# Element-wise work of a transformer kernel moved from GpSimd to the vector engine

## The chip, the cores and the metric

The kernel runs as one launch on one core of a Trainium2 chip. The core's engines work side by side, each through its own instruction queue: TensorE (PE) multiplies matrices, VectorE (DVE), ScalarE (ACT) and GpSimd (POOL) do element-wise work, and SyncE (SP) issues the weight transfers. The metric is the time of one execution in microseconds; several executions are told by their median, lowest and highest.

## The reference

Everything is float32, for 256 positions of width 1024. A first block has two layers `x + W_out(y)`, in which `y` joins four gated mixers (a 31-wide convolution, a 3-wide one, windowed attention, neighbourhood attention with a relative bias). A second block has two layers of feed-forward, mixing, feed-forward; its mixing joins a forgetting attention, a dilated attention and a gated recurrence (HGRN2). Cut to what the change touches:

```python
def rmsnorm(x, g):                       # before every stage
    y = x32 * lax.rsqrt(jnp.mean(x32 * x32, axis=-1, keepdims=True) + EPS)
y_b = short_gated_conv(b_b, b_c, b_x, conv_b_w) * jax.nn.silu(b_z)      # gate, one of four
scores = jnp.where(col_ok[:, None, :], scores + bias[None], NEG_INF)    # neighbourhood attention
out = jnp.concatenate([x1 * cos - x2 * sin, x2 * cos + x1 * sin, rest]) # rotary
def step(S, inp):                        # the recurrence, chunk by chunk
    q, k, v, lf = inp
    b = jnp.cumsum(lf, axis=2)
    D = jnp.exp(jnp.where(causal, b[:, :, :, None, :] - b[:, :, None, :, :], NEG_BIG))
    A = jnp.einsum('bhtse,bhse->bhts', q[:, :, :, None, :] * D, k)
    intra = jnp.einsum('bhts,bhsv->bhtv', A, v)
```

## The kernel before

Activations lie in SBUF with features on the 128 partitions and the 256 positions along the free axis; a width of 1024 is 8 slices of 128x256. Weights stream from HBM in pieces of up to 1 MB (`ws`) through SyncE's queue into three tiles `st`. To keep float32 accuracy on fp32r matmuls, each weight piece and each activation is split in a high and a low part, and every product is the sum of three matmuls (`hi` with `hi`, `hi` with `lo`, `lo` with `hi`). `hi` is an ACT copy of `st`. `lo` is either one DVE subtraction (`lo<-st,hi`, by `tt`), or ACT writes the negative of `hi` into `lo` and a DMA issued on POOL's queue (L592) adds `st` to it.

The stages follow each other: mixing of the first block (0 to 157 us and 157 to 298), then for each layer of the second block a feed-forward, a mixing and a feed-forward (298, 484, 640 and 826, 1010, 1166 to the end). A mixing is an input projection, element-wise work on its results, and an output projection.

**What sets the order.** The program is written as generators, each yielding operations (`Op`) and waits; a list scheduler (`Scheduler.step`) repeatedly takes the operation with the smallest estimated start, less a priority, by a table of costs of its own, and emits it. So each engine's instructions stand in one fixed order, and an engine waits at the instruction that is next. `V`, `A`, `G` put an operation on DVE, ACT, POOL; `tt`, `ts`, `stt` are DVE operations; `VG` allows DVE or POOL and leaves the choice to that estimate. Helpers emit everything, so that ACT's work is at L472, DVE's and POOL's at L495, the softmax's custom DVE operations at L526.

**What the change touches.**
- `prep`: the sum of squares for the next norm. Each of 8 slices is squared (`sq`, by ACT; on POOL before the first stage) and added to `sqa` (L805, `G`).
- `rope`: rotary, a product with `sinp` and an addition (`VG`).
- `biases` in the first block's mixing: the bias table `nb` is loaded, scaled by 8 (DVE), and a column mask is added (POOL), 4 times per layer.
- `z`: the gate's product `y` (`VG` where its coefficient is 1).
- `hf`: two subtractions of the forget gate (`VG`).
- `recurrence` and `level`: eight levels per layer. For each, ACT takes `e = exp(sp)` (tile `lev`, 128x1024), one of three buffers. Behind it two DVE additions update `sp` for the next level in place (`sp<-sp`, 128x512 each). Beside them `level` multiplies `lev` by `kq` (the product `lev<-lev,kq`, 128x1024, `VG`), PE forms small blocks from it (L546, for the last two levels L535), and DVE copies these into `at` under a mask (L1490, COPY_PREDICATED), ACT for the last levels. All eight done, PE forms the outputs from `at` and `hv`.

Round the recurrence stand, on the same engines, the forgetting attention (softmax tiles `pt`, with `fb`), the rotary (`u`, `ak`, `aq`), the dilated attention (its `pt` from `cst`), and the weights' splits.

Of the kernel before, what the change touches and what calls it, by code (L numbers as in the profile page):

```python
# [14 lines left out]
ALU = mybir.AluOpType  # L15
PSUM = bass.MemoryType.PSUM

P = 128
T = 256
# [380 lines left out]
class Builder:  # L400
# [380 lines left out]
    def prep(self, st, fo):  # L781

        yield self.xin[fo]
        xs = self.x[:, fo]
        g = st["g"][:, fo:fo + 1]
        if st["act"]:
            hi, lo, _ = st["pair"]
            yield self.A(hi[:, fo], xs, AF.Copy, scale=g)
            yield self.stt(lo[:, fo], xs, g, hi[:, fo].bitcast(F32), ALU.mult, ALU.subtract)
        st["ready"][fo].done = True  # L790
        if fo:
            yield st["summed"][fo - 1]
        for i, sc in enumerate(st["sq_scale"]):
            sq = yield (("sqa",) if fo == 0 else ("sq",))
            if st["first"]:
                yield self.G("tensor_tensor", sq, xs, xs, op=ALU.mult)
            else:
                yield self.A(sq, xs, AF.Square, scale=1.0 if sc is None else sc[:, fo:fo + 1])
            if fo == 0:
                st["acc"][i] = sq  # L800
            elif fo == KT - 1:
                st["last"][i] = sq
            else:
                a = st["acc"][i]
                yield self.G("tensor_tensor", a, a, sq, op=ALU.add)  # L805
                self.s.put("sq", sq)
        st["summed"][fo].done = True

# [219 lines left out]
    def rope(self, bank, ps, nf, cos, sin, o, tags):  # L1028


        s = self.s
        a, b = yield tags
        av, bv = a[:, :nf], b[:, :nf]
        for i in range(4):
            j = i ^ 1
            yield self.A(bv[32 * i:32 * i + 32], ps[32 * j:32 * j + 32], AF.Copy)
        yield self.tt(av, ps, cos[:, None, :].to_broadcast([P, nf, T]), ALU.mult)
        s.put("acc", bank)
        yield self.VG("tensor_tensor", bv, bv, sin[:, None, :].to_broadcast([P, nf, T]), op=ALU.mult)
        yield self.VG("tensor_tensor", o, av, bv, op=ALU.add)  # L1040
        s.put(tags[0], a)
        s.put(tags[1], b)


    def mix_a(self, l, st, nxt):
        nc, tc, s = self.nc, self.tc, self.s
        done = Event()
        with tc.tile_pool(name="mixa", bufs=1, reuse_waits="tile") as mp:
# [16 lines left out]
            def biases():  # L1065
                yield self.have_ct
                for b in range(2):
                    for h in range(4):
                        src = bass.AP(tensor=self.rpb.tensor,
                                      offset=self.rpb.offset + (l * 4 + h) * 465 + (5 - b) * 31 + 15 - 63,  # L1070
                                      ap=[[1, 64], [31, 6], [1, 64]])
                        yield self.DMA(nb[b * 64:b * 64 + 64, h], src, 98304)
                nb3 = nb.rearrange("p h u c -> p (h u) c")
                for h in range(4):
                    n1 = nb[:, h]
                    yield self.ts(n1, n1, 8.0, None, ALU.mult)
                    yield self.G("tensor_tensor", n1, n1, self.c["nacol"][:, None, :].to_broadcast([P, 6, 64]), op=ALU.add)
                E["bias"].done = True

            def small():  # L1080
# [144 lines left out]
            def z(o, ev, coef, k0, rev=False):  # L1225
                def f_(bank, ps):
                    th, gz = yield ("th", "gz")
                    yield self.A(th, ps, AF.Tanh, scale=0.5)
                    yield self.stt(gz, th, 1.0, ps, ALU.add, ALU.mult)
                    s.put("acc", bank)  # L1230
                    s.put("th", th)
                    yield E[ev]
                    y = yield ("y",)
                    for f in range(2):
                        a, b, c = y[:, f], o[:, f], gz[:, f]
                        if rev:
                            r = lambda q: q.rearrange("p (r c) -> p r c", c=64)
                            a, b, c = r(a), r(b)[:, :, ::-1], r(c)
                        if coef != 1.0:
                            yield self.stt(a, b, coef, c, ALU.mult, ALU.mult)  # L1240
                        else:
                            yield self.VG("tensor_tensor", a, b, c, op=ALU.mult)
                    s.put("gz", gz)
                    yield from emit(k0, y)
                    s.put("y", y)
                return f_
# [124 lines left out]
    def mix_b(self, l, st, nxt):  # L1371
        nc, tc, s = self.nc, self.tc, self.s
        done = Event()
        with tc.tile_pool(name="mixb", bufs=1, reuse_waits="tile") as mp:
# [42 lines left out]
            def hf(c):  # L1417
                def f_(bank, ps):
                    yield self.bconsts
                    h0 = 4 * l + 2 * c  # L1420
                    e, a = yield from log1p_exp(ps, 2, self.nlncol[:, h0:h0 + 2])
                    u, t1 = yield ("u", "u")
                    yield self.stt(u, ps, 0.0, a[:, 0], ALU.max, ALU.add)
                    yield self.stt(t1, ps, 0.0, a[:, 0], ALU.min, ALU.subtract)
                    for j in range(2):
                        h = 2 * c + j
                        yield self.A(kq[:, 0, h * T:h * T + T], u[:, j], AF.Exp, scale=-1.0,
                                     bias=self.l1mcol[:, h0 + j:h0 + j + 1])
                    for j in range(2):
                        yield self.ts(u[:, j], ps[:, j], self.lncol[:, h0 + j:h0 + j + 1], 0.0, ALU.subtract, ALU.min)  # L1430
                    s.put("acc", bank)
                    yield self.VG("tensor_tensor", u, u, a[:, 1], op=ALU.subtract)
                    s.put("lev", e)
                    yield self.VG("tensor_tensor", sp_[:, 1, c * 512:c * 512 + 512].rearrange("p (a b) -> p a b", a=2),
                                  t1, u, op=ALU.subtract)
                    s.put("u", u)
                    s.put("u", t1)
                    E[f"hf{c}"].done = True
                return f_
# [14 lines left out]
            def mixed(tl, m):  # L1454

                return bass.AP(tensor=tl.tensor, offset=tl.offset,
                               ap=[list(tl.ap[0]), [2 * m, D // (2 * m)], [D + m, 2], [1, m]])
# [22 lines left out]
            def level(lev, e):  # L1480
                m = 1 << lev
                ev = e.rearrange("p (b two m) -> p b two m", two=2, m=m)
                yield self.VG("tensor_tensor", ev, ev, mixed(kq, m), op=ALU.mult)
                bank = yield ("sm",)
                if m < 64:
                    for t in range(2):
                        yield blocks(bank, t, e, e)
                    yield box["lev"][lev]
                    mk = self.msk[:, lev * 64:lev * 64 + 64][:, None, :].to_broadcast([P, 8, 64])
                    yield Op([("V", .602, lambda: self.nc.vector.copy_predicated(atc, mk, b8(bank)))],  # L1490
                             [extent(atc)], [extent(bank), extent(self.msk)])
                    if m == 32:
                        for b in range(2):
                            bs = slice(64 * b, 64 * b + 64)
                            yield self.A(at[bs, 0:2, :, bs], atc[bs].rearrange("p (t h) j -> p t h j", t=2), AF.Copy)
                elif m == 64:
                    for h in range(4):
                        yield self.MMs([(b8(bank)[64 * t:64 * t + 64, h], e[:, h * T + t * P:h * T + t * P + 64],
                                         e[:, h * T + t * P + 64:h * T + t * P + P], True, True) for t in range(2)])
                    yield box["lev"][lev]  # L1500
                    for t in range(2):
                        yield self.A(at[:64, t, :, 64:], b8(bank)[64 * t:64 * t + 64, :4], AF.Copy)
                else:
                    pa = bank.rearrange("p (h t) -> p h t", h=4)
                    for h in range(4):
                        yield self.MM(pa[:, h], e[:, h * T:h * T + P], e[:, h * T + P:h * T + T])
                    yield box["lev"][lev]
                    yield self.A(at[:, 2], pa, AF.Copy)
                s.put("sm", bank)
                s.put("lev", e)  # L1510
                box["lev"][lev + 1].done = True
# [386 lines left out]
```

## Time and profile before

| | |
|---|---|
| median of 3 executions | 1361.81 us (1359.84 to 1370.74) |
| profiled execution | 1359.77 us, of which the span 1358.0 us |
| PE busy | 1277.9 us, 94% of the span |
| DVE busy | 865.0 us, 64%, 1481 instructions |
| ACT busy | 921.3 us, 68%, 1420 instructions |
| POOL busy | 320.1 us, 24%, 318 instructions |

The span runs from the first to the last instruction. The profile gives, for every instruction, start, duration, and what ended the idle time of its engine before it. A share of busy time is a mean over stages with different limits, so the stages have to be looked at one by one. A duration holds also time in which an instruction had started and could not go on, so that one operation of one shape can show very different durations.

### The profile page before, as it was taken

The numbers are of one execution on the slowest core, as the hardware profiler recorded it, in microseconds if no ns is written. First come the engines' busy times: TensorE is split into PE (matmuls) and PEld (weight loads), VectorE is DVE, ScalarE is ACT, GpSimd is POOL, SyncE is SP. The second block draws the span as 40 slices with busy tenths as digits, with TensorE's granted clock in tenths as the row PEclk, the third lists the DMA queues.
The fourth block names the chain that finished last, engine by engine and source line by source line (L and its number), as shares of the span: only waits on it lengthen the run. The fifth ranks groups of instructions, "written<-read, shape, count | busy, mean of one in ns | idle before, by whom it ended". The sixth has DMA issues, their size and how long they took to land.

```text
span 1358.0 us, 21863 instructions
## 1 busy us (share of the span) xinstructions
PE 1277.9 (94%) x8530; PEld 1144.4 (84%) x8530; DVE 865.0 (64%) x1481; ACT 921.3 (68%) x1420; POOL 320.1 (24%) x318
## 2 busy tenths in 40 slices
PE   6899988999999999789999999999999888999997
PEld 5888887888888898678888888888899776888886
DVE  6586658569966556856666556666555785666632
ACT  5487748777686578587666656666559767766652
POOL 4222312242121112512222112222121340322211
PEclk9899998999999999899999999999999899999998
DMA  8887988798777779255877777777778645877771
GB/s 262 229 234 203 231 237 232 204 241 271 224 235 240 236 219 256 82 171 156 263 233 234 228 230 228 225 240 237 239 232 230 180 104 161 236 243 242 236 226 53
DMA packets 59783, 294.09 MB, mean 217 GB/s; under 512 B 12448, under 2 KB 14240, under 8 KB 34208
## 3 DMA queue, kind: packets, MB, share of 16 engines
q1 hardware_dynamic: 39232, 219.01, 45.3%
q0 software_dynamic: 20448, 73.69, 28.5%
q8 instruction: 67, 1.10, 0.3%
q14 instruction: 36, 0.29, 0.1%
HBM read 217.94 MB, written 1.05 MB: 161 GB/s over the span
## 4 chain that ended last, share of the span: by engine, by line
PE 70%; ACT 10%; DVE 7%; DMA 7%; issue 3%; POOL 2%; SPq 0%; POOLq 0%; DVEq 0%; ACTq 0%
PE bank L576 34%; PE bank L577 19%; PE bank L579 4%; DMA lo<-st 3%; DVE sp L495 3%; ACT hi L472 3%; DMA st<-ws 3%; PE bank L563 2%; PE bank L565 2%; PE bank L564 2%; ACT lev L472 2%; PE bank L535 2%; ACT lo L472 1%; PE bank L546 1%; ACT pt L472 1%
## 5 line engine op out<-in xcount | busy, mean ns | idle before, releaser
L576 PE MATMUL bank<-act,hi 128*128 128x512 f32 x1456 | 520.0, 395 | 2.3 <-DVE act L495 2.3
L472 ACT ACTIVATE hi<-st 128x1024 fp32r<-128x1024 f32 (+3 forms) x416 | 428.6, 1036 | 80.6 <-DMA st<-ws 39.2
L577 PE MATMUL bank<-act,lo 128*128 128x256 f32 x1664 | 433.4, 281 | 0.6 <-ACT act L472 0.6
L495 DVE TENSOR_TENSOR lo<-st,hi 128x1024 fp32r<-128x1024 f32 (+1 forms) x274 | 338.0, 1237 | 133.5 <-ACT hi L472 130.1
L577 PEld LDWEIGHTS bank<-act,lo 128*128 128x128 f32 x1664 | 312.8, 188 | 18.6 <-ACT act L472 0.9
L576 PEld LDWEIGHTS bank<-act,hi 128*128 128x128 f32 x1456 | 273.6, 188 | 57.8 <-DVE act L495 3.8
L592 POOL DMA_DIRECT2D lo<-st x142 | 123.9, 873 | 652.2 <-ACT lo L472 524.1
L576 PE MATMUL bank<-ha,hi 128*128 128x512 f32 x672 | 236.7, 394 | 0.0
L565 PE MATMUL bank<-act,lo 128*128 128x256 f32 x720 | 208.9, 290 | 24.9 <-DMA lo<-st 24.9
L563 PE MATMUL bank<-act,hi 128*128 128x256 f32 x720 | 214.1, 297 | 0.0
L564 PE MATMUL bank<-act,hi 128*128 128x256 f32 x720 | 207.7, 288 | 0.0
L577 PE MATMUL bank<-ha,lo 128*128 128x256 f32 x704 | 192.7, 281 | 0.0
L565 PEld LDWEIGHTS bank<-act,lo 128*128 128x128 f32 x720 | 141.7, 197 | 26.1 <-DMA lo<-st 26.1
L472 ACT ACTIVATE lo<-hi 128x1024 fp32r<-128x1024 f32 (+1 forms) x142 | 149.3, 1052 | 3.8
L576 PEld LDWEIGHTS bank<-ha,hi 128*128 128x128 f32 x672 | 126.2, 188 | 27.0
L563 PEld LDWEIGHTS bank<-act,hi 128*128 128x128 f32 x720 | 142.1, 197 | 5.9 <-issue 5.0
L564 PEld LDWEIGHTS bank<-act,hi 128*128 128x128 f32 x720 | 141.4, 196 | 0.1
L577 PEld LDWEIGHTS bank<-ha,lo 128*128 128x128 f32 x704 | 132.4, 188 | 2.7
L495 POOL TENSOR_TENSOR fs<-fs,rbc 128x512 f32<-128x512 f32 x44 | 64.0, 1456 | 179.4 <-ACT fs L472 179.4
L495 DVE SCALAR_TENSOR_TENSOR x<-bank,x 128x256 f32<-128x256 f32 x128 | 53.6, 422 | 58.6 <-PE bank L579 56.7
L495 DVE TENSOR_TENSOR fh<-bank,fh 128x256 f32<-128x256 f32 x88 | 37.1, 423 | 76.6 <-ACT fh L472 76.6
L579 PE MATMUL bank<-act,hi 128*128 128x512 f32 x208 | 82.2, 395 | 0.1
(216 smaller groups left out, 1543.8 us busy)
## 6 DMA issues: line engine op xcount, KB each, us to landing
st<-ws SPq DMA_DIRECT2D x197, 1024.0 KB, 5.0
lo<-st POOLq DMA_DIRECT2D x136, 512.0 KB, 5.7
st<-ws SPq DMA_DIRECT2D x2, 1040.0 KB, 7.1
st<-ws SPq DMA_DIRECT2D x4, 512.0 KB, 7.4
st<-ws SPq DMA_DIRECT2D x8, 192.0 KB, 5.3
nb<-rpb SPq DMA_DIRECT2D x16, 96.0 KB, 7.5
st<-ws SPq DMA_DIRECT2D x2, 768.0 KB, 6.5
lo<-st POOLq DMA_DIRECT2D x2, 520.0 KB, 6.7
```

The costliest lines, as they stand in the source:

```text
L472: return Op([("A", dur, lambda: self.nc.scalar.activation(out, in_, func, **kw))], outs, ins, ACT_SETS.get(func))
L495: return (eng, dur, lambda: fn(out, *ins, **kw)), [extent(a) for a in aps]
L535: return Op([("P", dur, lambda: self.nc.tensor.matmul(out, lhsT, rhs, start=start, stop=stop))], [extent(out)], [extent(lhsT), extent(rhs)])
L546: mm(o, l, r, start=st, stop=sp)
L563: mm(out, ah, bh, start=first, stop=False)
L564: mm(out, ah, bl, start=False, stop=False)
L565: mm(out, al, bh, start=False, stop=last)
L576: mm(out, wh, x, start=first, stop=False)
L577: mm(out[:, 0], wl, x[:, 0], start=False, stop=False)
L579: mm(out, wh, x, start=False, stop=True)
L592: return Op([("G", ADD_ISSUE, lambda: self.nc.gpsimd.dma_start(out, src, accum_op=ALU.add))], [extent(out)], [extent(src), extent(out)], l ...
```

## The change

Five places name DVE where GpSimd or the scheduler's choice stood, and the table's two operations become one (`stt`: times 8, plus mask).

```diff
--- before.py
+++ after.py
@@ -802,7 +802,7 @@
                 st["last"][i] = sq
             else:
                 a = st["acc"][i]
-                yield self.G("tensor_tensor", a, a, sq, op=ALU.add)
+                yield self.tt(a, a, sq, ALU.add)
                 self.s.put("sq", sq)
         st["summed"][fo].done = True
 
@@ -1036,8 +1036,8 @@
             yield self.A(bv[32 * i:32 * i + 32], ps[32 * j:32 * j + 32], AF.Copy)
         yield self.tt(av, ps, cos[:, None, :].to_broadcast([P, nf, T]), ALU.mult)
         s.put("acc", bank)
-        yield self.VG("tensor_tensor", bv, bv, sin[:, None, :].to_broadcast([P, nf, T]), op=ALU.mult)
-        yield self.VG("tensor_tensor", o, av, bv, op=ALU.add)
+        yield self.V("tensor_tensor", bv, bv, sin[:, None, :].to_broadcast([P, nf, T]), op=ALU.mult)
+        yield self.V("tensor_tensor", o, av, bv, op=ALU.add)
         s.put(tags[0], a)
         s.put(tags[1], b)
 
@@ -1073,8 +1073,7 @@
                 nb3 = nb.rearrange("p h u c -> p (h u) c")
                 for h in range(4):
                     n1 = nb[:, h]
-                    yield self.ts(n1, n1, 8.0, None, ALU.mult)
-                    yield self.G("tensor_tensor", n1, n1, self.c["nacol"][:, None, :].to_broadcast([P, 6, 64]), op=ALU.add)
+                    yield self.stt(n1, n1, 8.0, self.c["nacol"][:, None, :].to_broadcast([P, 6, 64]), ALU.mult, ALU.add)
                 E["bias"].done = True
 
             def small():
@@ -1239,7 +1238,7 @@
                         if coef != 1.0:
                             yield self.stt(a, b, coef, c, ALU.mult, ALU.mult)
                         else:
-                            yield self.VG("tensor_tensor", a, b, c, op=ALU.mult)
+                            yield self.V("tensor_tensor", a, b, c, op=ALU.mult)
                     s.put("gz", gz)
                     yield from emit(k0, y)
                     s.put("y", y)
@@ -1429,9 +1428,9 @@
                     for j in range(2):
                         yield self.ts(u[:, j], ps[:, j], self.lncol[:, h0 + j:h0 + j + 1], 0.0, ALU.subtract, ALU.min)
                     s.put("acc", bank)
-                    yield self.VG("tensor_tensor", u, u, a[:, 1], op=ALU.subtract)
+                    yield self.V("tensor_tensor", u, u, a[:, 1], op=ALU.subtract)
                     s.put("lev", e)
-                    yield self.VG("tensor_tensor", sp_[:, 1, c * 512:c * 512 + 512].rearrange("p (a b) -> p a b", a=2),
+                    yield self.V("tensor_tensor", sp_[:, 1, c * 512:c * 512 + 512].rearrange("p (a b) -> p a b", a=2),
                                   t1, u, op=ALU.subtract)
                     s.put("u", u)
                     s.put("u", t1)
@@ -1480,7 +1479,7 @@
             def level(lev, e):
                 m = 1 << lev
                 ev = e.rearrange("p (b two m) -> p b two m", two=2, m=m)
-                yield self.VG("tensor_tensor", ev, ev, mixed(kq, m), op=ALU.mult)
+                yield self.V("tensor_tensor", ev, ev, mixed(kq, m), op=ALU.mult)
                 bank = yield ("sm",)
                 if m < 64:
                     for t in range(2):
```

Counted over the whole program, DVE has 80 instructions more and POOL 88 fewer. From POOL to DVE go 60 sums `sqa<-sqa,sq`, 16 level products and 5 gate products `y`; 8 scalings and 8 additions of `nb` become 8 DVE instructions. The rotary's operations and the two of `hf` stood on DVE already. One product of the feed-forward's gate (`fg<-fg,rbc`), which the scheduler may place, goes to POOL. The 8 first squares stay on POOL. PE's and SP's counts are the same; ACT loads its function table twice more, in the feed-forward that starts at 298 us. Since the scheduler's estimates change, the order changes also around the moved work.

POOL, first recurrence (`lev_n` is one of the three buffers, `st`, `hi`, `lo` the weights'), before:

```order
L592 DMA lo_78<-st_72 128x1024
L495 TENSOR_TENSOR lev_4397<-lev_4397,kq 128x1024
L495 TENSOR_TENSOR lev_4398<-lev_4398,kq 128x1024
L495 TENSOR_TENSOR lev_4396<-lev_4396,kq 128x1024
L592 DMA lo_79<-st_73 128x1024
L495 TENSOR_TENSOR lev_4397<-lev_4397,kq 128x1024
L495 TENSOR_TENSOR lev_4398<-lev_4398,kq 128x1024
L495 TENSOR_TENSOR lev_4396<-lev_4396,kq 128x1024
```

The same stretch of POOL now:

```order
L592 DMA lo_79<-st_73 128x1024
L592 DMA lo_77<-st_72 128x1024
L592 DMA lo_78<-st_71 128x1024
L592 DMA lo_79<-st_73 128x1024
L592 DMA lo_77<-st_72 128x1024
```

The eight products are gone, and POOL holds nothing but the accumulating DMAs.

DVE, first recurrence, from the third pair of additions (`sc` and `pt` belong to the forgetting attention's softmax), before:

```order
L495 TENSOR_TENSOR sp<-sp 128x128x4 x2
L495 TENSOR_SCALAR pt_4407<-pt_4407,sc_102 128x128
L495 TENSOR_SCALAR pt_4407<-pt_4407,sc_102 128x256
L526 ISA pt_4409,sc_103<-bank_117,fb 128x128
L526 ISA sc_103 128x1
L526 ISA pt_4409,sc_103<-bank_117,fb 128x256
L526 ISA sc_103 128x1
L495 RECIPROCAL sc_105<-sc_105 128x4
L495 TENSOR_SCALAR pt_4408<-pt_4408,sc_105 128x128
L495 TENSOR_SCALAR pt_4408<-pt_4408,sc_105 128x256
L495 TENSOR_TENSOR act_81<-bank_121,act_81 128x256
L495 TENSOR_SCALAR pt_4409<-pt_4409,sc_105 128x128
```

The same now:

```order
L495 TENSOR_TENSOR sp<-sp 128x128x4 x2
L495 TENSOR_SCALAR pt_4401<-pt_4401,sc_102 128x128
L495 TENSOR_SCALAR pt_4401<-pt_4401,sc_102 128x256
L526 ISA pt_4403,sc_103<-bank_117,fb 128x128
L526 ISA sc_103 128x1
L526 ISA pt_4403,sc_103<-bank_117,fb 128x256
L526 ISA sc_103 128x1
L495 TENSOR_TENSOR lev_4391<-lev_4391,kq 128x1024
L495 RECIPROCAL sc_105<-sc_105 128x4
L495 TENSOR_SCALAR pt_4402<-pt_4402,sc_105 128x128
L495 TENSOR_SCALAR pt_4402<-pt_4402,sc_105 128x256
L495 TENSOR_TENSOR lev_4392<-lev_4392,kq 128x1024
```

The first two products (`lev_4391`, `lev_4392`) stand behind the third pair and inside the softmax; the products of the later levels follow between the next pairs in the same way.

ACT, the last exponentials (`lev<-sp`) of the first recurrence, before:

```order
L472 ACTIVATE pt_4409<-bank_117 128x128
L472 ACTIVATE lev_4397<-sp 128x1024
L472 ACTIVATE act_81<-bank_116 128x256
L472 ACTIVATE lev_4398<-sp 128x1024
L472 ACTIVATE lev_4396<-sp 128x1024
L472 ACTIVATE u_4400<-bank_118 32x512 x2
L472 ACTIVATE lev_4397<-sp 128x1024
L472 ACTIVATE u_4400<-bank_118 32x512 x2
L472 ACTIVATE lev_4398<-sp 128x1024
L472 ACTIVATE hi_74<-st_71 128x1024 x2
```

Now, with `pt` and `sc` here those of the dilated attention:

```order
L472 ACTIVATE pt_4401<-bank_121 128x256
L472 ACTIVATE pt_4401<-bank_121 128x128
L472 ACTIVATE pt_4402<-bank_116 128x256
L472 ACTIVATE pt_4402<-bank_116 128x128
L472 ACTIVATE lo_79<-hi_76 128x1024
L472 ACTIVATE act_81<-bank_120 128x256
L472 ACTIVATE pt_4403<-bank_117 128x256
L472 ACTIVATE pt_4403<-bank_117 128x128
L472 ACTIVATE lev_4391<-sp 128x1024
L472 ACTIVATE act_81<-bank_116 128x256
L472 ACTIVATE lev_4392<-sp 128x1024
```

The five exponentials of levels 3 to 7 stood close together and ahead of all of the dilated attention's softmax. Now the last two stand behind it: exponential 5 (`lev_4390`) stands 25 rows ahead of the first of them, and the softmax's instructions and copies are between. On DVE too the dilated softmax stands ahead of the seventh pair of additions and of the last two products.

## Rows read from the trace of the kernel before

**Rows 1.** The page: span, and each engine's busy time, share and instructions.
```profile
span 1358.0 us, 21863 instructions
...
PE 1277.9 (94%) x8530; PEld 1144.4 (84%) x8530; DVE 865.0 (64%) x1481; ACT 921.3 (68%) x1420; POOL 320.1 (24%) x318
```

**Rows 2.** The page: shares of the chain that ended last, by line.
```profile
PE bank L576 34%; PE bank L577 19%; PE bank L579 4%; DMA lo<-st 3%; DVE sp L495 3%; ACT hi L472 3%; DMA st<-ws 3%; PE bank L563 2%; PE bank L565 2%; PE bank L564 2%; ACT lev L472 2%; PE bank L535 2%; ACT lo L472 1%; PE bank L546 1%; ACT pt L472 1%
```

**Rows 3.** Busy time of each engine in five stretches, with PE's granted clock and DMA share.
```profile
core 0: us, PE busy (x) PEld busy (x) DVE busy (x) ACT busy (x) POOL busy (x), PEclk, DMA share, GB/s
537.00:614.00 77.00, 60.28 (x588) 52.98 (x585) 56.74 (x96) 50.98 (x105) 26.84 (x12) 0.91 0.46 131
548.00:552.00 4.00, 3.77 (x20) 3.48 (x18) 3.97 (x7) 1.10 (x6) 2.66 (x1) 0.53 0.39 166
566.00:582.00 16.00, 11.17 (x131) 10.23 (x132) 14.71 (x12) 9.62 (x12) 10.31 (x5) 0.89 0.07 26
640.00:770.00 130.00, 130.00 (x749) 114.00 (x748) 82.96 (x116) 89.96 (x130) 26.36 (x23) 1.00 0.79 241
1063.00:1140.00 77.00, 60.24 (x587) 52.98 (x586) 56.78 (x97) 51.11 (x105) 26.89 (x12) 0.91 0.45 133
```

**Rows 4.** PE's timeline: start, duration, instruction, idle time before it and its releaser.
```profile
33.56 0.58 PE L565 MATMUL bank<-act,lo 128*128 128x256 f32 x1 [5.84 <-DMA lo<-st]
...
547.08 0.95 PE L553 MATMUL bank<-cst,pt 128*128 128x128 f32 x3 [5.37 <-DVE pt L495]
...
566.88 1.15 PE L546 MATMUL bank<-lev 128*64 128x64 f32 x32 [1.35 <-POOL lev L495]
...
571.53 1.43 PE L546 MATMUL bank<-lev 128*64 128x64 f32 x32 [1.88 <-POOL lev L495]
...
580.89 1.16 PE L535 MATMUL bank<-lev 128*128 128x128 f32 x8 [1.69 <-POOL lev L495]
...
602.14 0.49 PE L535 MATMUL bank<-at,hv 128*128 128x128 f32 x2 [3.06 <-ACT at L472]
...
610.58 1.12 PE L535 MATMUL bank<-u,ones 128*128 128x512 f32 x2 [1.00 <-ACT kq L472]
...
613.55 0.50 PE L576 MATMUL bank<-act,hi 128*128 128x512 f32 x1 [1.13 <-DVE act L495]
```

**Rows 5.** DVE's timeline: a mixing's end (144), and the first recurrence (538 to 547).
```profile
144.67 2.22 DVE L495 SCALAR_TENSOR_TENSOR act<-x,par,act 128x256 fp32r<-128x256 f32 x2
...
538.04 3.80 DVE L495 TENSOR_TENSOR sp<-sp 128x512 f32<-128x512 f32 x2
...
543.09 3.52 DVE L495 TENSOR_TENSOR sp<-sp 128x512 f32<-128x512 f32 x2
...
546.73 0.55 DVE L495 TENSOR_SCALAR pt<-pt,sc 128x128 f32<-128x128 f32 x2
```

**Rows 6.** DVE's groups by line and shape, whole run: busy us, mean ns, idle before.
```profile
L495 DVE TENSOR_TENSOR lo<-st,hi 128x1024 fp32r<-128x1024 f32 x260 | 325.2, 1253 | 127.1 <-ACT hi L472 123.7 <-PE bank L576 2.8
...
L495 DVE TENSOR_TENSOR sp<-sp 128x512 f32<-128x512 f32 x28 | 48.8, 1744 | 4.3 <-ACT lev L472 3.4
...
L495 DVE TENSOR_TENSOR y<-bc,gz 128x256 f32<-128x256 f32 x4 | 1.5, 423 | 0.1
```

**Rows 7.** POOL's groups, whole run.
```profile
L495 POOL TENSOR_TENSOR sqa<-sqa,sq 128x256 f32<-128x256 f32 x60 | 50.8, 850 | 118.6 <-ACT sq L472 117.6
L495 POOL TENSOR_TENSOR lev<-lev,kq 128x1024 f32<-128x1024 f32 x16 | 46.8, 2923 | 25.6 <-ACT lev L472 25.6
...
L495 POOL TENSOR_TENSOR nb<-nb,cst 128x384 f32<-128x384 f32 x8 | 9.4, 1181 | 7.2 <-DVE nb L495 7.2
```

**Rows 8.** Tile `sp`: additions on DVE, exponentials on ACT; duration ns min/median/max, first and last start.
```profile
L495 DVE TENSOR_TENSOR sp<-sp x28: 691/1707/3073, 538.0 to 1100.0; 128x512 f32<-128x512 f32 x28
L472 ACT ACTIVATE lev<-sp x16: 1058/1062/1527, 536.5 to 1102.8; 128x1024 f32<-128x1024 f32 x16
```

**Rows 9.** POOL's line 592, issuing the accumulating DMAs: ns min/median/max.
```profile
L592 POOL DMA_DIRECT2D lo<-st x142: 846/872/1037, 27.3 to 1330.6; - x142
```

## The prediction

> **What bounds the kernel now.** I read the page's busy shares first: PE is busy 94% of the span, no other engine over 68% [rows 1]. Matmuls lead the chain that ended last; of its element-wise work, DVE's `sp` has 3% and ACT's `lev` 2%, both parts of the recurrence, and the DMA into `lo` 3% [rows 2]. Then I read the stretches. In a feed-forward PE is busy 130.00 of 130 us, with DVE at 82.96 and POOL at 26.36 [rows 3]: nothing that this change does to DVE or POOL there can gain, and work of DVE has some 47 us of room. The recurrences differ: of 77 us from 537, and again from 1063, PE is busy 60.28 and 60.24, at a mean clock of 0.91, with the DMA engines at 0.46 and 0.45 [rows 3]. Here PE waits for DVE, POOL and ACT, and most of the change lies here. The two stretches are alike to 0.2%, so I work out one and double it.
>
> PE's idle times there [rows 4]: 5.37 us until 547.08 for a product of the softmax (`pt`) on DVE; then 1.35, 1.88 and 1.69 for POOL's level products; then 3.06, 1.00 and 1.13 behind ACT and DVE as the recurrence's outputs are formed. These make 15.5 of the 16.7 idle us.
>
> The next view is DVE's own. The `pt` product of 546.73 stands behind two pairs of additions that took 3.80 and 3.52 us [rows 5]. The 28 additions average 1.744 us, the cheapest takes 0.691, the longest 3.073 [rows 6, 8]. So a pair could take 1.4; it takes some 2.1 more, about as long as POOL's 2.923 us product beside it still runs [rows 7]. Each additional microsecond makes ACT's next exponential later, and that the next product. I take the stretching to come from POOL's product; the trace has no pair without one that would prove it.
>
> **The change, part by part** (us; the profiled execution's 1359.8 is the base; the median of the runs is 2.0 above it).
>
> *Level products, per recurrence.* Removed: 8 POOL operations of 2.923. Added: 8 on DVE. The nearest DVE row is the weights' subtraction, also 128x1024 from two SBUF operands, 1.253 [rows 6]. Added to DVE 8 x 1.253 = 10.0; taken off, if the stretching goes, 14 x (1.744 - 0.691) = 14.7. DVE's own load in the stretch so falls slightly, 56.74 to about 52, and does not become the bound. From both sides for a product: not under 0.691 (an addition, half the elements), not over POOL's 2.923. I take 1.253, since engine, size and operand count agree. A level's operands are strided by powers of two; ACT's exponentials over the same layouts take 1.06, one of them 1.53 [rows 8], so the first product may cost half a microsecond more. [...] The trace speaks against it on DVE: the first pair hops in the same way and took 3.80, of which the longest addition can fill 3.07 [rows 5, 8], which leaves 0.73 for the other.
>
> What PE gains per recurrence:
> - The 5.37 wait. Both pairs ahead of `pt` shrink by 3.80 - 1.4 and 3.52 - 1.4, together 4.5; the first two products now stand behind the third pair, so they add nothing ahead of it. I take 4.5; bounds 2.1 (one pair shrinks) and 5.37.
> - The three waits for POOL's products, 4.92. A level's period was an exponential (1.06) and a stretched pair (3.5), 4.6 together. It becomes 1.06, a pair at 1.4 and a product at 1.25, 3.7, which is 0.85 less for each of five levels. I take 3.6; bounds 0 (other DVE work fills in) and 4.9.
> - PE's clock. [...] With the idle times mostly gone I take back 2.5; bounds 0 and 3.1.
> - The end, 5.2 of waits. The last two exponentials and products now come behind the dilated attention's softmax on ACT and DVE. That softmax was itself behind all levels in the old order, and comes earlier now. I take a gain of 2; bounds -6 (an exponential, two products and a pair put behind everything: 1.06 + 2 x 1.25 + 1.4 = 5.0, and a microsecond of semaphores) and +4.
>
> Sum 4.5 + 3.6 + 2.5 + 2 = 12.6 per recurrence, 25.2 for two.
>
> *Sums of squares.* 60 operations leave POOL at 0.850 and reach DVE at the price of the same shape, 0.423 [rows 6, 7]: 25.4 us of DVE. About half lie in feed-forwards, covered by PE's full load; if that cover were gone, 13 us would show. In the output projections they also compete with the evictions. There DVE's pair of `act` operations took 2.22 us beside POOL's sums [rows 5], against 0.423 for a two-operand operation of that shape [rows 6]. I set 0; bounds +4 and -2 for all of them. At the start six sums now stand between DVE's first weight splits: 6 x 0.423 = 2.5 us, while less of DVE's work there is stretched. PE's first long wait, 5.84 at 33.56 [rows 4], ends with a DMA into `lo`, not with DVE. I take a loss of 1; bounds -4 and +1.
>
> *Bias table, gates, rotary.* The table loses 8 POOL operations of 1.181 [rows 7] and keeps one DVE operation for each; five gates move at 0.423. All of it stands well ahead of its reader or beside PE's work: 0; bounds -1 and +1. Rotary and `hf` stood on DVE already: 0. The moved feed-forward product and the table loads lie under PE's full load: 0.
>
> Total: 1359.8 - 25.2 + 1 = 1335.6, which I give as **1336**. The bounds of the recurrence, 2.1 + 0 + 0 - 6 = -4 to 5.4 + 4.9 + 3.1 + 4 = 17 each, are not met together; the least I hold plausible is 4 and the most 18.
>
> **The rivals.**
> 1. *The wait moves.* DVE takes over the products but they queue with the dilated softmax and the splits, and the last levels' exponentials come later. Then only the first wait and some clock remain, and the end loses: 4.5 + 2 - 0.5 = 6 each, 1359.8 - 12 = **1348**. For it: the order of ACT and DVE at the end. Against it: DVE has 20 us of idle time in 77 [rows 3].
> 2. *Slower: DVE becomes the recurrence's bound.* If a product takes POOL's time on DVE too (2.9), and the additions do not shrink since strides and not POOL stretch them, DVE's work is 56.74 + 8 x 2.9 = 80 of 77 us, plus the waits inside, so each recurrence grows by some 7: 1359.8 + 14 + 1 = **1375**. The point of decision is DVE work of some 70 us, beyond which its queue alone sets the end: products over 1.7 us with unshrunk additions, or over 3.5 with shrunk ones. Against it: one addition of a pair takes 0.69 to 0.73 with the same strides [rows 5, 8].
> 3. *Given back at the weights.* PE's earlier start of the next stages finds weights late, or the accumulating DMAs that POOL issues suffer from DVE's added two-operand work. By rows, an issue takes 0.872 at the median and 1.037 at most [rows 9], although DVE is busy 64% of the span: 0.17 for each of some six waits on `lo`, 1 us. A shift of the start by one full wait per layer (5.84) costs 12: **1348**. Against it: a DMA share of 0.46 in the recurrence [rows 3]. [...]
>
> **How the numbers follow.** Chances: the forecast 0.60 (1325 to 1342), more than that 0.06, rival 1 0.20 (1342 to 1354), rival 2 0.07, rival 3 0.07. The predicted time is the likeliest case's, 1336. The range goes down to 1322 (18 each, and a gain of 1 at the start) and up to 1352, to take in rivals 1 and 3 for the most part; about 2 in 10 stay outside. A measurement of this kernel can tell about 1% from no change, that is 1348.2 and 1375.4 round the median. Faster by over 1%: 0.60 + 0.06 and half of rivals 1 and 3, 0.79. Slower by over 1%: half of rival 2 and mishaps, 0.05. Within 1%: 0.16.
>
> **What would show it.** DVE's `sp<-sp` pairs at 1.4 us; the level products on DVE near 1.25, the first at most 1.8; PE's wait before the softmax's matmuls under 2 us; PE's clock at 1.0 through the recurrence; each recurrence stretch 10 to 16 us shorter, and the feed-forwards of the same length. I am wrong if the additions stay at 3.5 without a product on POOL, if DVE is busy nearly all through the recurrence, if PE's wait for `at` near the end grows past 8 us, or if a stage's first matmuls wait longer for `lo`.

## The result, and the profile after

The changed kernel takes 1343.84 us (median of 4, 1343.04 to 1345.7) against 1363.62 (median of 4, 1359.84 to 1370.74): a ratio of 0.9858, 95% interval 0.983 to 0.9886. That is 1.4% faster, 19.8 us by the medians. The profiled executions, 1359.77 and 1343.41, differ by 16.4, where the sum was 24.2; the steps below are sized on these two.

The page after, span, busy shares and the chain by line:

```profile
span 1341.6 us, 21822 instructions
...
PE 1278.4 (95%) x8530; PEld 1140.2 (85%) x8530; DVE 853.3 (64%) x1561; ACT 920.5 (69%) x1422; POOL 212.0 (16%) x230
...
DMA st<-ws 15%; PE bank L576 14%; DMA lo<-st 14%; PE bank L577 8%; ACT hi L472 6%; DVE lo L495 3%; ACT lo L472 3%; PE bank L563 3%; PE bank L565 3%; PE bank L564 3%; PE bank L535 2%; PE bank L546 2%; ACT lev L472 2%; PE bank L579 1%; PE bank L553 1%
```

POOL lost 108 us of its 320, DVE did 80 instructions more in 12 us less. The chain that ended last now runs through the weight transfers (`st<-ws` and `lo<-st`, 29% together) where it ran through the matmuls [rows 2]. That does not mean that PE waits more for its weights: its idle times that end with a transfer into `lo` were 24.9 us in all and are 23.2, and a run below that is as fast (sums back on GpSimd) has 68% of its chain on PE.

The stretches that answer to [rows 3], the recurrences and a feed-forward:

```profile
core 0: us, PE busy (x) PEld busy (x) DVE busy (x) ACT busy (x) POOL busy (x), PEclk, DMA share, GB/s
527.00:598.00 71.00, 60.20 (x635) 52.93 (x633) 52.04 (x108) 54.90 (x110) 4.31 (x5) 0.93 0.56 160
581.00:598.00 17.00, 9.28 (x31) 6.58 (x30) 5.45 (x10) 9.64 (x19) 0.00 (x0) 0.70 0.18 63
640.00:770.00 130.00, 129.89 (x744) 113.36 (x743) 79.55 (x114) 85.66 (x122) 25.33 (x22) 1.00 0.77 230
1047.00:1119.00 72.00, 61.43 (x636) 53.42 (x634) 51.71 (x107) 55.20 (x110) 4.34 (x5) 0.91 0.55 159
1119.00:1127.00 8.00, 7.16 (x33) 6.25 (x34) 3.23 (x7) 4.56 (x7) 0.86 (x1) 0.76 0.13 27
```

PE's idle times in the first recurrence, answering to [rows 4] (start, duration, instruction, idle time and releaser):

```profile
536.73 0.70 PE L553 MATMUL bank<-cst,pt 128*128 128x128 f32 x3 [0.93 <-DVE pt L495]
...
566.42 0.33 PE L553 MATMUL bank<-cst,pt 128*128 128x128 f32 x1 [0.95 <-DVE pt L495]
...
584.92 0.79 PE L535 MATMUL bank<-at,hv 128*128 128x128 f32 x2 [3.83 <-ACT at L472]
...
589.63 2.07 PE L535 MATMUL bank<-u,ones 128*128 128x512 f32 x2 [1.17 <-ACT kq L472]
...
595.28 1.13 PE L535 MATMUL bank<-u,ones 128*128 128x512 f32 x2 [1.23 <-ACT kq L472]
...
598.25 0.50 PE L576 MATMUL bank<-act,hi 128*128 128x512 f32 x1 [1.49 <-DVE act L495]
```

The 5.37 us wait is 0.93, the waits for level products are gone, one of 0.95 for the dilated softmax is new. But the wait for `at` at the end has grown from 3.06 to 3.83, and those behind it too.

DVE, answering to [rows 5, 6, 8]: the additions' tile, the groups of sums and products, and from the timeline two pairs, the softmax product and the first level product.

```profile
L495 DVE TENSOR_TENSOR sp<-sp x28: 684/693/694, 532.1 to 1095.5; 128x512 f32<-128x512 f32 x28
```

```profile
L495 DVE TENSOR_TENSOR sqa<-sqa,sq 128x256 f32<-128x256 f32 x60 | 25.3, 426 | 9.9 <-ACT sq L472 9.4
L495 DVE TENSOR_TENSOR lev<-lev,kq 128x1024 f32<-128x1024 f32 x16 | 19.9, 1257 | 0.0
```

```profile
532.13 1.42 DVE L495 TENSOR_TENSOR sp<-sp 128x512 f32<-128x512 f32 x2
...
534.80 1.42 DVE L495 TENSOR_TENSOR sp<-sp 128x512 f32<-128x512 f32 x2
...
536.39 0.55 DVE L495 TENSOR_SCALAR pt<-pt,sc 128x128 f32<-128x128 f32 x2
...
539.70 1.53 DVE L495 TENSOR_TENSOR lev<-lev,kq 128x1024 f32<-128x1024 f32 x1
```

All 28 additions take 0.684 to 0.694 now; each pair fell from 3.5 to 1.4. The products take 1.257 on average, the first of a recurrence 1.53, the sums 0.426.

A stage is measured here from one norm to the next, by the last of the matmuls (`ones,sq`) with which PE sums the squares for it. The first block and feed-forward 1 are taken together, since the new order puts some 20 of PE's matmuls on the other side of the boundary between them. Lengths in us, with PE's idle time in brackets:

| stage | before | after |
|---|---|---|
| first block and feed-forward 1 | 481.16 (35.9) | 475.93 (30.4) |
| mixing with recurrence 1 | 156.67 (18.8) | 146.32 (11.1) |
| feed-forwards 2 and 3 | 370.83 (0.0) | 373.44 (1.0) |
| mixing with recurrence 2 | 155.29 (17.5) | 149.43 (11.5) |
| feed-forward 4 | 186.47 (1.4) | 189.09 (2.8) |

So the recurrences gave 16.2 us, the part ahead of them 5.2, and the feed-forwards behind them took 5.2 back, of which 2.4 is idle time of PE. The rest lies in PE's busy time, at a granted clock of 1.00 in both kernels and for as many matmuls to within two.

### The profile page after: what moved, and what is told of

Read it like the earlier page. It is cut to its first block, busy times and chain, and to the rows that moved or that the text cites. A ratio compares the mean times of both kernels' runs of the same rounds, so it can differ in the third digit from the quotient of the medians.

```text
span 1341.6 us, 21822 instructions
## 1 busy us (share of the span) xinstructions
PE 1278.4 (95%) x8530; PEld 1140.2 (85%) x8530; DVE 853.3 (64%) x1561; ACT 920.5 (69%) x1422; POOL 212.0 (16%) x230
## 3 DMA queue, kind: packets, MB, share of 16 engines
HBM read 217.94 MB, written 1.05 MB: 163 GB/s over the span
## 4 chain that ended last, share of the span: by engine, by line
PE 38%; DMA 29%; ACT 16%; DVE 10%; issue 6%; SPq 1%; POOL 0%; DVEq 0%; POOLq 0%; ACTq 0%
DMA st<-ws 15%; PE bank L576 14%; DMA lo<-st 14%; PE bank L577 8%; ACT hi L472 6%; DVE lo L495 3%; ACT lo L472 3%; PE bank L563 3%; PE bank L565 3%; PE bank L564 3%; PE bank L535 2%; PE bank L546 2%; ACT lev L472 2%; PE bank L579 1%; PE bank L553 1%
## 5 line engine op out<-in xcount | busy, mean ns | idle before, releaser
L495 DVE TENSOR_TENSOR lo<-st,hi 128x1024 fp32r<-128x1024 f32 (+1 forms) x274 | 330.7, 1212 | 166.2 <-ACT hi L472 162.9
L565 PE MATMUL bank<-act,lo 128*128 128x256 f32 x720 | 206.9, 287 | 19.9 <-DMA lo<-st 19.8
L563 PE MATMUL bank<-act,hi 128*128 128x256 f32 x720 | 211.4, 294 | 0.0
L564 PE MATMUL bank<-act,hi 128*128 128x256 f32 x720 | 205.3, 285 | 0.0
```

What stands on the lines that cost most here:

```text
L495: return (eng, dur, lambda: fn(out, *ins, **kw)), [extent(a) for a in aps]
L563: mm(out, ah, bh, start=first, stop=False)
L564: mm(out, ah, bl, start=False, stop=False)
L565: mm(out, al, bh, start=False, stop=last)
```

## The experiments

Theory A: GpSimd's product held up the additions beside it, and taking it away is the gain. Theory B: the sums' move (in the table's run, B2: the table's) is, through the first block. Theory C: any edit shifts the time through the scheduler's order alone. Four runs do one part of the change each, in the kernel before.

**Only the level products.**

```diff
-                yield self.VG("tensor_tensor", ev, ev, mixed(kq, m), op=ALU.mult)
+                yield self.V("tensor_tensor", ev, ev, mixed(kq, m), op=ALU.mult)
```

> The kernel before with only the sixteen level products moved to the vector engine. Theory A (the products on GpSimd stretch the additions beside them, and that is where the gain comes from): additions 0.69 each, each recurrence stage 6 to 10 us shorter, first block unchanged within 1 us, in all 12 to 18 us faster (about 1345 to 1350). Theory B (the scheduler's new order in the first block, made by the sums, gives most of it): 5 us or less faster. Theory C (any single edit shifts the time by several us through the order alone): no relation.

Measured: 1348.28 us (6 runs), ratio 0.9902 (0.988 to 0.9923). The recurrence stages take 147.18 and 148.58, the first part 482.12. Its additions (tile `sp`, ns min/median/max):

```profile
L495 DVE TENSOR_TENSOR sp<-sp x28: 685/693/694, 539.1 to 1103.0; 128x512 f32<-128x512 f32 x28
```

Theory A holds for the recurrences: 16.2 us shorter together, as much as in the changed kernel, and no gain ahead of them. It holds for the whole too: 1.0% is 13 us, of the 12 to 18 expected. That is less than 16.2, since feed-forwards 2 and 3 took 375.22 (3.4 idle) and feed-forward 4 188.21: 6 us went back.

**Only the sums.**

```diff
-                yield self.G("tensor_tensor", a, a, sq, op=ALU.add)
+                yield self.tt(a, a, sq, ALU.add)
```

> The kernel before with only the sixty sums of squares moved to the vector engine. Theory A: the recurrences unchanged within 1 us, additions still 1.74 on average, whole within 3 us of before. Theory B: the first block 4 to 5 us shorter, as in the changed kernel (155.0 to 150.9 and so on), whole 4 to 6 us faster. If the sums also make the feed-forwards wait for their weights, each feed-forward gets 1 to 2 us longer here too.

Measured: 1359.47, ratio 0.9975 (0.9947 to 1.0002). First part 480.94, recurrence stages 157.56 and 155.00. The first block alone ends 7.5 us earlier, but feed-forward 1 takes 7.2 us more. Not Theory B's 4 to 6 us: alone the sums are worth 3 us or nothing.

**Only the table.**

```diff
-                    yield self.ts(n1, n1, 8.0, None, ALU.mult)
-                    yield self.G("tensor_tensor", n1, n1, self.c["nacol"][:, None, :].to_broadcast([P, 6, 64]), op=ALU.add)
+                    yield self.stt(n1, n1, 8.0, self.c["nacol"][:, None, :].to_broadcast([P, 6, 64]), ALU.mult, ALU.add)
```

> The kernel before with only the bias table made in one vector instruction instead of two. Theory A: within 1 us of before. Theory B2 (the table's loads and its GpSimd additions stand ahead of accumulating DMAs in the first block, whose late landings PE waits for): first block 2 to 5 us shorter, the rest unchanged.

Measured: 1361.52, ratio 0.9982 (0.996 to 1.0005); the first part took 478.98, 2.2 less, the rest is unchanged. The interval can't tell it from nothing.

**Only the gates.**

```diff
-                            yield self.VG("tensor_tensor", a, b, c, op=ALU.mult)
+                            yield self.V("tensor_tensor", a, b, c, op=ALU.mult)
```

> The kernel before with only the gate products fixed to the vector engine. Theory A and B: within 1 us of before. Theory C: several us either way.

Measured: 1361.6, ratio 0.9992 (0.997 to 1.0014): nothing, though single stages moved by 1 to 3 us (recurrence 1 at 159.37, feed-forward 4 at 189.13, the first part at 479.90). The four ratios' distances from 1 add up to 1.5%, the changed kernel has 1.4%.

Two runs take a part back out of the changed kernel. **The products back with the scheduler**, which puts them on GpSimd:

```diff
-                yield self.V("tensor_tensor", ev, ev, mixed(kq, m), op=ALU.mult)
+                yield self.VG("tensor_tensor", ev, ev, mixed(kq, m), op=ALU.mult)
```

> The changed kernel with the level products left to the scheduler again, which puts all sixteen on GpSimd: sums, table and gates alone are moved. Theory A: additions at 1.74 on average again, PE's 5.37 us wait is back, recurrence stages at 155 to 157 us, feed-forwards behind them at 185.4; whole 1352 to 1360.

Measured: 1358.05, ratio 0.9964 (0.9939 to 0.9989), recurrence stages 159.52 and 157.06 (155 to 157 expected), and the additions are as before:

```profile
L495 DVE TENSOR_TENSOR sp<-sp x28: 691/1708/3190, 536.9 to 1101.5; 128x512 f32<-128x512 f32 x28
```

So sums, table and gates together are worth 0.4%, some 5 us, and the products 1.0%. (The first part takes 476.89, 4.3 less than before.) **The sums back on GpSimd:**

```diff
-                yield self.tt(a, a, sq, ALU.add)
+                yield self.G("tensor_tensor", a, a, sq, op=ALU.add)
```

> The changed kernel with the sums of squares back on GpSimd, so products, table and gates alone moved. Theory A: recurrences as in the changed kernel, additions at 0.69. If the sums are worth 3 to 4 us (as they measured alone), 1346 to 1348; if they are worth nothing, 1343 to 1345.

Measured: 1344.39, ratio 0.9867 (0.9852 to 0.9883), against 0.9858 with them moved: here the sums are worth nothing that can be told.

**Does a GpSimd operation hold the additions, and which kind?** The changed kernel with four useless GpSimd operations beside each level; `scr` is never read.

```diff
                     yield self.A(ev, mixed(sp_, m), AF.Exp)
+                    yield self.G("tensor_tensor", scr, e[:, 0:256], e[:, 256:512], op=ALU.mult)
+                    for i in range(1, 4):
+                        yield self.G("tensor_tensor", scr, kq[:, 0, 256 * i:256 * i + 256], kq[:, 1, 256 * i:256 * i + 256], op=ALU.mult)
```

> The changed kernel with four products of 128x256 on GpSimd beside each level, from SBUF into a scratch tile that nothing reads. Theory A (an addition that meets a GpSimd product is held until that product ends): additions over 0.69 again, each held by up to the 0.7 to 0.85 us of one short product, so a mean of 1.0 to 1.4. Rival (the stretching came from the level product's own data or strides): additions stay at 0.69.

Measured (one execution): 1350.77. The additions' group (busy us, mean ns), and one level in the timeline:

```profile
L495 DVE TENSOR_TENSOR sp<-sp 128x512 f32<-128x512 f32 x28 | 26.1, 931 | 0.5
```

```profile
550.92 2.70 POOL L495 TENSOR_TENSOR scr<-kq 128x256 f32<-128x256 f32 x3
...
552.07 2.10 DVE L495 TENSOR_TENSOR sp<-sp 128x512 f32<-128x512 f32 x2
```

The mean rose from 0.692 to 0.931. It is below the 1.0 expected, since not every addition met a product. Both sides wait: the pair took 2.10 in place of 1.4, and the three products 2.70, where the shortest of their kind is 0.73 each. The recurrence stages take 153.58 and 154.01, where the changed kernel has 146.32 and 149.43: work that nothing reads costs most of what the change gave there. In the second run the last three operations only write:

```diff
-                        yield self.G("tensor_tensor", scr, kq[:, 0, 256 * i:256 * i + 256], kq[:, 1, 256 * i:256 * i + 256], op=ALU.mult)
+                        yield self.G("memset", scr, 0.0)
```

> As the run with four short GpSimd products beside each level, but three of the four only write (a fill of the scratch tile with zero), and one reads. If an addition is held only by a GpSimd operation that reads SBUF, its mean falls well below the 0.98 to 1.03 of four products, to 0.75 to 0.85; if any GpSimd operation holds it, it stays near 0.9 to 1.0.

Measured (one execution): 1335.32.

```profile
L495 DVE TENSOR_TENSOR sp<-sp 128x512 f32<-128x512 f32 x28 | 19.6, 701 | 0.5
L495 DVE TENSOR_TENSOR sp<-sp x28: 669/690/1101, 534.5 to 1085.4; 128x512 f32<-128x512 f32 x28
```

```profile
549.41 0.73 POOL L495 TENSOR_TENSOR scr<-lev 128x256 f32<-128x256 f32 x1 [0.20 <-ACT lev L472]
...
550.20 1.39 DVE L495 TENSOR_TENSOR sp<-sp 128x512 f32<-128x512 f32 x2
550.20 1.05 POOL L495 MEMSET scr<- 128x256 f32 x3
```

Three fills run 1.05 us right beside a pair, and the pair takes 1.39: not held. The mean of 0.701, lower than I expected, leaves nothing for the fills: of the nine additions that met one, eight took 0.67 to 0.69, and the ninth, of 1.10, met a product as well. So GpSimd's products, which read SBUF, held vector additions with two SBUF operands (0.931 on average, 0.692 in the changed kernel), and its fills, which only write, did not (0.701). That this run is also the fastest of all by its one time is not the fills' doing as far as can be shown: the added operations change the scheduler's order (recurrence stages 145.01 and 143.69).

**Is the end of the recurrence a matter of order?**

```diff
-            conv=0.3, att=1.8, evac=1.1, level=0.3, prep=-0.7, rec=2.3, bias=-1.3, vg=0.2)
+            conv=0.3, att=1.8, evac=1.1, level=2.3, prep=-0.7, rec=2.3, bias=-1.3, vg=0.2)
```

> The changed kernel with the scheduler's priority of the recurrence's levels raised from 0.3 to 2.3, so that the last exponentials, additions and copies into `at` come ahead of the dilated attention's softmax. Theory: at the end of each recurrence PE waits because the levels' last copies stand behind other work of ACT (3.83 us for `at`, and three waits of 1.2 to 1.5). Then PE's wait for `at` falls under 1 us and each recurrence stage gets 2 to 5 us shorter, at most 10 us in all, unless the feed-forward behind it gives it back by waits for `lo`. Rival: the softmax becomes the last work and PE waits for it as long; time as before, 1342 to 1346.

Measured: 1341.44 (4 runs), ratio 0.9841 (0.9796 to 0.9886), not to be told from the changed kernel. PE's idle times in the first recurrence's second half:

```profile
578.60 0.49 PE L546 MATMUL bank<-ak,aq 64*128 64x128 f32 x4 [2.34 <-DVE aq L495]
...
583.98 0.70 PE L553 MATMUL bank<-cst,pt 128*128 128x128 f32 x3 [1.67 <-DVE pt L495]
...
604.11 0.51 PE L577 MATMUL bank<-act,lo 128*128 128x256 f32 x2 [2.22 <-DMA lo<-st]
```

The waits for `at` are gone, and PE waits for the dilated attention (`aq`, `pt`) and a weight instead. The two stages take 150.21 and 145.51, 295.7 together, against 295.75. The rival was right in kind (1342 to 1346 expected): whichever comes last is waited for.

**The feed-forwards.** Landings in feed-forward 2, from 640 to 800 us (instruction count, KB, median us from issue to landing), before:

```profile
st<-ws SPq DMA_DIRECT2D x29, 1024.0 KB, 4.8
lo<-st POOLq DMA_DIRECT2D x15, 512.0 KB, 4.8
```

and after:

```profile
st<-ws SPq DMA_DIRECT2D x29, 1024.0 KB, 5.3
lo<-st POOLq DMA_DIRECT2D x14, 512.0 KB, 9.7
```

The accumulating DMAs, which landed in 4.8 us at the median, take 9.7. With only the products moved it is the same, in the run of the first experiment, and PE waits for them (its longest idle time there):

```profile
st<-ws SPq DMA_DIRECT2D x30, 1024.0 KB, 7.1
lo<-st POOLq DMA_DIRECT2D x14, 512.0 KB, 9.5
```

```profile
641.32 0.39 PE L577 MATMUL bank<-act,lo 128*128 128x256 f32 x1 [1.84 <-DMA lo<-st]
```

But they can be late without a shorter recurrence. With the products back with the scheduler they are nearly as late, behind a recurrence stage of 159.52, and PE never waits for them in that feed-forward:

```profile
lo<-st POOLq DMA_DIRECT2D x14, 512.0 KB, 9.4
```

And with only the gates moved, feed-forward 4 has them at 9.4 behind a recurrence stage of 154.91, and PE waits 1.9 us for them there.

In the next kernel DVE makes every low part in the feed-forwards:

```diff
-SHARE_F = 0.25
+SHARE_F = 0.0
```

> The changed kernel with no accumulating DMAs for the feed-forwards' low parts: the vector engine subtracts all of them (the share of 0.25 set to 0; POOL issues 69 instead of 142). Theory G (the feed-forwards give back 5 us, since their loads and accumulating DMAs run into each other when PE comes early: landings of 7.8 to 9.7 us instead of 5): PE's idle time in the feed-forwards falls to that of before, they take 185.4 us each again, 3 to 6 us faster. Rival: the vector engine's 18 more subtractions of 1.22 us per feed-forward delay evictions and splits, and the feed-forwards get longer: no gain or slower.

Measured: 1338.55, ratio 0.9827 (0.9806 to 0.9849). The feed-forwards behind the recurrences take 371.72 and 185.77 (373.44 and 189.09 in the changed kernel), and the loads land in 4.8 us in each of them. That is 5.0 us less given back. In feed-forward 2, 0.98 us of waiting for `lo` is left. The first part is 4.2 shorter too (471.70), and recurrence 1, at 151.43, takes 5.1 of it away.

The same edit in the kernel before:

> The kernel before with no accumulating DMAs for the feed-forwards' low parts. If what this share cost in the changed kernel is only the work given back after a shorter recurrence, the feed-forwards here stay at 185.4 us each and the whole within 3 us of before. If the share costs time of itself, 4 to 6 us faster here too.

Measured: 1354.01, ratio 0.9925 (0.9899 to 0.995). This falls outside both readings: it is 9.5 us faster, though its profiled feed-forwards are those of before (370.85 and 186.51). Its profiled execution took 1358.1 us from first to last instruction and is the slowest of its five, so the profile does not show where the others gained. The share costs time in both kernels, then, and not only after a shorter recurrence.

**Both edits**, the levels' priority and `SHARE_F`, in the changed kernel.

> The changed kernel with the levels' priority at 2.3 and no accumulating DMAs in the feed-forwards. If the two gains are separate, 1333 to 1337; if the priority's gain was only order, 1338 to 1341.

Measured: 1339.47, ratio 0.9826 (0.9799 to 0.9854): the priority adds nothing to the share. By medians the share alone is the fastest timed version that I can offer, 1338.55 against 1343.84 and 1363.62; its interval overlaps that of the changed kernel, so that step is likely and not settled.

Each kernel was profiled once, so a stage's length by itself can be off by a few us. Taken together they show the products' part: a recurrence stage takes 153.9 to 159.5 us in the six kernels that have them on GpSimd, and 145.5 to 151.4 in the six that have them on DVE with nothing added.

## Why the prediction was right, point by point

The time was forecast at 1336 and is 1343.84. That is inside the stated range (1322 to 1352), but above the 1325 to 1342 of the likeliest case: it falls where rival 1 (0.20) was put, and the end of the recurrence lost time, as in rival 1, though its three waits for products went. The upper bound of 18 a recurrence, behind the 1322, is more than the prediction's own bounds add up to, 17.4.

- *The additions.* Right in mechanism and size: 3.5 to 1.4 a pair. That GpSimd's product caused it was an assumption there; the runs with short products (0.931 an addition on average) and with fills (0.701) show it.
- *The product on DVE.* 1.253 was taken, 1.257 measured on average: 1.53 for the first of a recurrence, 1.218 at the median. So the first costs 0.3 more than the others, once a layer, where half a microsecond more was held possible from ACT's exponentials. The argument that the first pair of additions showed no stride cost holds for the additions (0.684 to 0.694 at every level) and did not carry over to the product: an addition of the first pair steps by two words, while the first product takes its `kq` operand by turns from the tile's two halves. That this difference is the cause, no run shows.
- *The 5.37 wait.* 4.5 taken, 4.44 measured. *The three waits for products.* 3.6 taken; 4.92 gone and 0.95 new, so 4.0.
- *The clock.* 2.5 a layer was taken, a term that no run shows by itself; what shows is PE's busy time in the stage, which fell by 2.6 in layer 1 and rose by 0.15 in layer 2. At the end, where PE's waits grew, the granted clock was 0.70 in 581 to 598 and 0.76 in 1119 to 1127; the stretches that answer to these before, 597 to 614 and 1140 to 1148, had 0.90 and 1.00. The 1.0 through the recurrence that was named as a sign did not come (0.93 and 0.91).
- *The end of the recurrence* failed, in sign: a gain of 2 a layer was taken, and its waits rose from 5.5 to 8.0 us, a loss of 2.5. The microsecond of semaphores in its lower bound was the author's estimate, and no run shows it. ACT shows why the waits rose:

```profile
578.21 1.04 ACT L472 ACTIVATE hi<-st 128x1024 fp32r<-128x1024 f32 x1
...
579.93 0.60 ACT L472 ACTIVATE lev<-bank 128x512 f32<-128x512 f32 x1
580.56 1.29 ACT L472 ACTIVATE lev<-lev 128x512 f32<-128x512 f32 x2
581.75 1.04 ACT L472 ACTIVATE hi<-st 128x1024 fp32r<-128x1024 f32 x1
...
583.31 1.29 ACT L472 ACTIVATE lev<-lev 128x512 f32<-128x512 f32 x2
584.51 1.39 ACT L472 ACTIVATE at<-bank 64x256 f32<-64x256 f32 x3
```

  PE had its last level blocks done at 581.09. The copy into `at` starts at 584.51, behind what is left of the output gate's work (`lev<-bank`, `lev<-lev`) and a weight split (`hi<-st`). The prediction had named the dilated softmax as what would stand ahead, and it was not the last thing that did. So each recurrence gave 10.35 and 5.86 instead of 12.6.
- *Sums, table, gates.* A loss of 1 was taken, a gain of 5.2 in the first part is there in the profile, and 0.4% in the runs. It does not come from one of them: the sums alone gave 0.2 of it, the table 2.2, the gates 1.3, all three without the products 4.3, and the sums taken back out leave 2.4. PE's longest idle times there are waits for accumulating DMAs: the one of 5.84 [rows 4] is 6.70 now, another of 5.99 is 3.87. How much of it is GpSimd's freed queue and how much another order stays open. The sums held vector work too: the 56 `act` operations fell from 0.638 to 0.484 us on average, 8.2 us of DVE, and with the sums back on GpSimd they take 0.636 again. That run is as fast, so PE was not waiting for them.
- *Feed-forwards.* Set at 0, under PE's full load; 5.2 us went back there. This was rival 3 in kind, given a chance of 0.07: PE finds its weights late. In feed-forward 2 the five profiled kernels with the products on GpSimd and a share of 0.25 have no wait for `lo`, and the six with them on DVE wait 0.2 to 2.7 us for it. That the accumulating DMAs are late is shown by the landings, and that PE waits for them by its idle times. But rival 3's reason, PE's earlier start, is not shown: they land nearly as late (9.4) behind two recurrences that are not shorter, and feed-forward 3 of the changed kernel has them at 9.7 with 0.1 us of waiting. Why they are late stays open.

So 16.4 of the 24.2 us came: the recurrences gave 9.0 less than forecast, the first part 6.2 more, and the feed-forwards took 5.2 back. The errors partly cancel; the recurrences alone were forecast half too large.

## What to carry to other kernels

An element-wise operation can cost the vector engine time while it runs on GpSimd. Here DVE took on 19.9 us of products, and its additions became 29.4 shorter (48.8 to 19.4). Look for one shape at two durations on DVE, and for a GpSimd operation that reads SBUF at the longer ones. Before forecasting that a wait goes, list what else stands ahead of the waited-for instruction on its own engine; here the waits at the end grew though the additions ahead of them were faster. And a stage in which PE is fully busy need not stay so: set its transfers' landings beside those of the kernel before, since with only the products moved they became twice as long in feed-forward 2 (4.8 to 9.5 us), where that edit changes no operation.

## What the runs showed of the hardware that was not expected

GpSimd's fills (0.313 us for 128x256) ran beside vector additions without holding them (0.67 to 0.69 for eight of nine that met one), while its products of the same size did (0.931 on average over all 28), and were held themselves: 0.73 us alone, up to 1.99 when they met vector work. Vector operations with one operand in a matmul's `bank` were not held: in the kernel before, 58 of `x<-bank,x` and `fh<-bank,fh` met a GpSimd product and took at most 0.43 us, as the others did. An operation on one SBUF tile and a column, `pt<-pt,sc`, was held: 0.77 us beside a product of the run with four, 0.29 alone.

Accumulating DMAs of 512 KB landed in 4.8 or in 9.7 us at the median, at nearly the same share of traffic (0.79 and 0.77 of the DMA engines' time).
